# A decoder layer on one core: the last gate/up pair in the wide form, the third block sum behind a split, and turned rows and the last differential head placed later

## Chip, core and metric

The kernel runs on one core of a Trainium2 chip. The metric is the device time of one execution in microseconds (us), the median of three runs. One further execution was taken by the hardware profiler; the profile and the trace are of that one.

## What is computed

One layer, float32, 256 rows of 2048 channels: a half-step SwiGLU feed-forward network (FFN1), a mixer with two attention branches (multi-head latent attention, MLA, with 8 heads, and differential attention with 4 heads), an output projection, and a second FFN. LayerNorm follows each part. Cut to what matters here:

```python
D_MODEL, SEQ, D_FF = 2048, 256, 5632

def _swiglu(x, w_gate, w_up, w_down):
    return (jax.nn.silu(x @ w_gate) * (x @ w_up)) @ w_down

def _mixer(h, ...):
    c_q, c_kv, k_r, dq, dk, dv, gate_mla, gate_diff = _split_columns(h @ w_in)
    q = (_rms_norm(c_q, q_norm_g) @ w_uq)        # 8 heads, 128 plain + 64 turned by _rope
    k_nope, v_mla = c_kv @ w_uk, c_kv @ w_uv     # c_kv after _rms_norm
    o_mla = _mla_attention(q, k, v_mla)          # softmax(q k^T) v, causal
    o_diff = _diff_attention(dq, dk, dv, positions, lam)   # (softmax1 - lam * softmax2) v
    y = sigmoid(gate_mla) * (o_mla @ w_br_mla) + sigmoid(gate_diff) * (o_diff @ w_br_diff)
    return y @ w_out
```

## The kernel before

**Products in three parts.** TensorE (PE) multiplies in a reduced float32 format, so every operand is split in a high and a low part (`split`, L156): ScalarE (ACT) casts the high part (L158), VectorE (DVE) subtracts it for the low part (L159). One product of 128x128 by 128x512 is three matmuls (`triple`, L211: high by high L212, high by low L213, low by high L214). The split weights lie in a ring of six pairs of tiles named `wring`. A unit of work has a load, a preparation (its splits) and its products; loads are issued three units and preparations four units ahead of the products (`look(3, 4)`). `later(n, f)` puts a piece of other work n units behind. The scheduler then decides each engine's order; `tc.issue_after(i)` only keeps an instruction behind another in the order and adds no wait.

**Gate/up.** Each FFN's gate and up weights come in 11 pairs of column blocks of 512, over 16 k tiles of 128. Pair 0 is computed plainly. Pairs 1 to 10 are handled by `Hybrid`: k tiles 0 to 7 are multiplied by a form with seven products in place of eight, which needs sums of weight blocks (DVE, L466, `sraw<-sraw,sraw`; two further sums are made by accumulating DMAs of POOL, L468 and L473) and adds combinations of the activations (tiles `xs`, `xe`, `xm`). The seven products are called forms 1 to 7; forms 6 and 4 need sums on DVE. Each form comes in block 0 and block 1 (two k tiles each) and a third block. In a "narrow" pair the third block is one more k tile (128x512), in a "wide" pair two (128x1024), so that k tiles 8 to 11 too go by seven products. The rest of the k tiles is plain (`p` and `q` units, two k tiles each). The order of forms and plain units is one line of a table:

```python
    ORDERS = {0: "pp5p36np27q4qqq", 1: "p5p36np27q4qq", 2: "5p36np27q4q"}
    PLAIN = {0: ((8, 9), (10, 11), (12, 13), (14, 15)), 1: ((9, 11), (12, 13), (14, 15)), 2: ((12, 13), (14, 15))}
```

(n is form 1 of the next pair). Before the change pairs 2, 3, 4, 6, 7 and 8 are wide. The sum of block 0 is issued with block 0, those of blocks 1 and 2 with block 1, each pinned behind a split already in line (`behind_split`).

**Down.** The gated products `hb` are transposed on DVE in 32x32 blocks (`turn_out`, L771), written to DRAM (`hT`, L773, POOL) and read back as `hraw`; those of pairs 3, 4 and 0 are read back by the SP queue during pair 10 (`get_half`, L1016), and split into `h`. The down projection follows in a similar mixture of sliced forms and plain units.

**Mixer.** Rows are turned to columns through DRAM in the same way: `turn` writes blocks, `wait` units later reads them back (`turned`), and `more` units later uses them; `turn_to_cols` copies with ACT (L795), `turn_to_quad` splits. `qr_done` does this for the rotary part of MLA's q (`qrT`). A differential head has four steps: scores with softmax (L1257 and L1258 are the exponentials, L748 is a square root), `turn` (PE transposes p, L1268), `values`, and `turn2`. Their places among the projections' units are set by `later(2 + 5 * h + 3 * i + i // 3, f)` (L1459). The exponential and the square root lie in different tables of ACT, so changing from one to the other loads a table.

Of the kernel before, what the change touches and what calls it, by code (L numbers as in the profile page):

```python
# [23 lines left out]
KF = DFF // P  # L24
# [4 lines left out]
DH = 4  # L29
# [30 lines left out]
def layer_kernel(ctx: ExitStack, tc: tile.TileContext, a: dict, out: bass.AP):  # L60
# [6 lines left out]
    small = ctx.enter_context(tc.tile_pool(name="small", bufs=1))  # L67
# [4 lines left out]
    def nm(s):  # L72
        uid[0] += 1
        return f"{s}_{uid[0]}"

    def act_tile(shape, dt=F32, name="act"):
        return apool.tile(shape, dt, tag="act", name=nm(name), bufs=SLOTS)

    def tmp_tile(shape, name="tmp", dt=F32):
        return small.tile(shape, dt, tag="tmp", name=nm(name), bufs=6)  # L80
# [26 lines left out]
    def later(n, fn):  # L107
        uid[0] += 1
        heapq.heappush(todo, (step[0] + n, uid[0], fn))
# [45 lines left out]
    cast, lows, fetched, placed, weights = [None], [None], [None], [None], [None]  # L155
# [42 lines left out]
    def unit(load, prep, now, later_on=None):  # L198
        if load is not None:
            load()  # L200
        loaded.append((prep, now, later_on))
        advance(*ahead)

    def next_pair():
        assert len(ring) > len(prepared) + lag[0], (len(ring), len(prepared), lag[0])
        catch_up(len(ring) - 1)
        pair = ring.pop(0)
        ring.append(pair)
        return pair

    def triple(o, xh, xl, wh, wl, first, last, again=False):  # L211
        PE.matmul(o, xh, wh, start=first, stop=False, skip_group_check=again)  # L212
        PE.matmul(o, xh, wl, start=False, stop=False, skip_group_check=again)  # L213
        PE.matmul(o, xl, wh, start=False, stop=last, skip_group_check=again)  # L214
# [139 lines left out]
    def behind_split(n):  # L354
        return tc.issue_after(line[-n].ins) if len(line) >= n else nullcontext()

    def split_in_line(strict, *a):
        with behind_split(1) if strict else nullcontext():
            line.append(split(*a))

    class Hybrid:
# [42 lines left out]
        def group(self, w0, w1, done, wide=0, seeded=False, gates=False):  # L404
            banks = {}
            small = self.small
# [22 lines left out]
            def bank(n):  # L429
                first = n not in banks  # L430
                if first:
                    banks[n] = tr_bank() if n == "Z" and not small else mm_bank()
                return banks[n], first
# [9 lines left out]
            def source(name, s):  # L443
                w, j0 = blocks[name]
                return w[j0 + s] if s < 2 else w[4 + j0 // 2][:, :wide * 512]

            def stored(name, s):
                return R[name][s] if s < 2 else R[name][s][:, :wide * 512]

            def seventh(p, s):  # L450
                load_block, src, add, b = plan[p]
                st = {}
                tiles = G if s < 2 else wide

                def load():
                    if s < 2 and load_block in there:
                        return
                    nc.sync.dma_start(stored(load_block, s), source(load_block, s))

                def prep():  # L460
                    t = stored(src, s)
                    last = None
                    if add is not None:
                        for i in {0: (0,), 1: tuple(range(1, end_s + 1)), 2: ()}[s]:
                            with nullcontext() if small else behind_split(s + 1):
                                last = V.tensor_tensor(out=stored(src, i), in0=stored(src, i), in1=stored(add[1], i), op=ALU.add)  # L466
                    if p == 6 and p in added:
                        nc.gpsimd.dma_start(stored("22", s), source("12", s), accum_op=ALU.add)  # L468
                    pair = [v[:, :tiles * 512] for v in next_pair()]
                    with tc.issue_after(last.ins) if last is not None and not small else nullcontext():  # L470
                        split_in_line(not small, *pair, t)
                    if p == 1 and p in added:
                        nc.gpsimd.dma_start(stored("11", s), source("12", s), accum_op=ALU.add)  # L473
                    st["pair"] = [v.rearrange("p (g n) -> p g n", g=tiles) for v in pair]

                def now():
                    o, first = bank(b)
                    wh, wl = st["pair"]
                    for g in range(tiles):
                        if s < 2:  # L480
                            xh, xl = (v[:, 2 * s + g, :] for v in self.seven.at_[p])
                        else:
                            xh, xl = (v[:, g, :] for v in self.extra.at_[p])
                        triple(o, xh, xl, wh[:, g, :], wl[:, g, :], first and g == 0,
                               s == end_s and g == tiles - 1 and p in stops, b in "XZ" or seeded)
                    if s == end_s and p in after:
                        after[p]()
                unit(load if load_block else None, prep, now)
# [42 lines left out]
            turn = {n: iter(PLAIN[wide]) for n in range(2)}  # L531
# [236 lines left out]
    def turn_out(row, to):  # L768

        t = tmp_tile([P, 512], "blocks")  # L770
        V.transpose(t, row)  # L771
        for i in range(4):
            nc.gpsimd.dma_start(to.rearrange("(g r) (i f) -> i r g f", g=4, i=4)[i],  # L773
                                t[32 * i:32 * (i + 1), :].rearrange("r (g f) -> r g f", g=4))

    def turned(v):
        return v.rearrange("p (i k c) -> p k i c", i=4, k=4)

    def turn(row, use, wait, more):
        to = dram.tile([P, 512], F32, name=nm("turn"))  # L780
        turn_out(row, to)

        def back():
            t = tmp_tile([P, 512], "turned")
            nc.gpsimd.dma_start(t, to)
            later(more, lambda: use(turned(t)))
        later(wait, back)

    def turn_to_quad(row, b, x, q, wait, more):
        turn(row, lambda t: x.put(q, b, t), wait, more)  # L790

    def turn_to_cols(row, dst, b, wait, more, pinned=False):
        def use(t):
            with tc.issue_after(cast[0].ins) if pinned else nullcontext():
                S.copy(dst[:, :, b * P:(b + 1) * P].rearrange("p k (i c) -> p k i c", i=4), t)  # L795
        turn(row, use, wait, more)
# [167 lines left out]
    def ffn(n, x, wgu, wdn, residual, g, bt, each, first=None, between=None, nxt=None, cols=None, norm=None, pending=None):  # L964
# [32 lines left out]
        def sum_done(c, b, bank, snap, op):  # L997
            if snap is None:
                gu_done(c, b, bank)
                return  # L1000
            t = tmp_tile([P, 512], "gus")
            V.tensor_tensor(out=t, in0=bank, in1=snap, op=op)
            half(c, b, t[:, 256:512], t[:, 0:256], 1)
# [60 lines left out]
        def begin():  # L1064
            hy = Hybrid(x, seven, KD, extra=extra, early=early)
            hybrid.append(hy)
            hy.plan([(wgu[2 * p], wgu[2 * p + 1],
                      lambda n, b, bank, snap, op, p=p: sum_done(2 * p + n, b, bank, snap, op),
                      2 if p in (2, 3, 4, 6, 7, 8) else 1, p > 1, ask if p == KF // 4 - 1 else lambda: None)
                     for p in range(1, KF // 4)])  # L1070
        project(wgu[0], x, KD, 512, lambda b, bank: gu_done(0, b, bank), hook=first_hook,
                between=between, norm=norm)
# [17 lines left out]
        for p in range(2):  # L1090
# [30 lines left out]
            else:  # L1121
                call(len(units) - 8, widen)
            down.run(wdn[2 * p], wdn[2 * p + 1], units, forms,
                     lambda m, b, bank, sign, p=p: ln.fold(2 * p + m, b, bank, sign),
                     lambda m, b, bank, p=p: ln.evac(2 * p + m, b, bank), calls, 8 * p)
# [162 lines left out]
    def mixer(x, norm):  # L1288
# [47 lines left out]
        def cols_proj(w, xx, kt, name, k0=0, more=4, pinned=False):  # L1336
            dst = act_tile([P, 4, T], F32, name)

            def done(b, bank):
                t = tmp_tile([P, 512], name + "r")  # L1340
                S.copy(t, bank)
                later(1, lambda: turn_to_cols(t, dst, b, 4, more, pinned))
            project(w, xx, kt, 512, done, k0)
            return dst
# [111 lines left out]

        for h in range(DH):
            for i, f in enumerate(diff_head(h)):
                later(2 + 5 * h + 3 * i + i // 3, f)  # L1459
        qT = [cols_proj(a["wuq"][c], cn, 4, "qT") for c in range(2)]  # L1460
        qrT = act_tile([P, 4, T], F32, "qrT")

        def qr_done(b, bank):
            t = tmp_tile([P, 512], "qr")
            tv = t.rearrange("p (j h i) -> p j h i", j=2, h=MH)
            rope(tv[:, 0], tv[:, 1], bank, b, MH)
            later(1, lambda: turn_to_cols(t, qrT, b, 4, 4))
        project(a["wuq"][2], cn, 4, 512, qr_done)
        kT = [cols_proj(a["wuk"][c], cn, 4, "kT", 4, 6, True) for c in range(2)]
        v = [act_tile([P, 1024], F32, "v") for _ in range(2)]  # L1470
# [211 lines left out]
```

## Time and profile before

| what | us |
|---|---|
| median of 3 runs (lowest to highest) | 1958.54 (1957.15 to 1961.01) |
| the profiled execution, its own time | 1957.34 |
| its span in the trace | 1955.6 |
| PE busy | 1943.0 |
| DVE busy | 1760.4 |
| ACT busy | 1276.4 |
| POOL busy | 377.0 |

The trace gives each instruction its start, its duration and, in brackets, how long its engine had been idle before it and what ended that. Some neighbouring instructions of one line are printed as one row with a count (x3). PE's matmuls are pipelined: each is shown with about 0.39 us, and the next starts before it ends, so what counts there is the distance from start to start. The granted clock of PE was 1.00 throughout. In the order of time, FFN1's gate/up pairs end near 445, its down projection follows, the mixer's attention heads stand between about 1020 and 1110, and FFN2's pair 4 ends near 1471.

### The profile page before, as it was taken

Reading aid. Unit: us, or ns where it says so; the run is one execution under the profiler, and the core shown is the slowest. Engines: PE = TensorE matmul, PEld = TensorE weight load, DVE = VectorE, ACT = ScalarE, POOL = GpSimd, SP = SyncE. Lnnn points to the kernel's source line nnn. Section 1 sums busy time; section 2 is a strip of 40 time slices with the busy share of each in tenths; the row PEclk is TensorE's granted clock in tenths of the full one; section 3 lists DMA queues with packets and bytes.
Section 4 is the critical chain, followed back from the end, with each engine's and each line's share of the span. In section 5 each row is a group of like instructions: output and inputs, shape, how many; then the busy total and the mean of one; then the engine's idle time right before and its main releaser. Section 6 shows DMA issues by size and latency. Waiting matters only on the chain.

```text
span 1955.6 us, 25740 instructions
## 1 busy us (share of the span) xinstructions
PE 1943.0 (99%) x8715; PEld 1609.0 (82%) x8715; DVE 1760.4 (90%) x2117; ACT 1276.4 (65%) x1636; POOL 377.0 (19%) x610
## 2 busy tenths in 40 slices
PE   9999999999999999999999999999999999999998
PEld 8888888888888888888888888888888888888886
DVE  7999999999898879988987677789999999998987
ACT  6677676776655666666667655566767676666652
POOL 0122212321100010102241530012221122210110
PEclk9999999999999999999999999999999999999999
DMA  9988997988877667767676798688988888888973
GB/s 333 295 239 244 271 303 236 239 269 279 313 245 240 215 218 269 262 201 241 198 260 203 221 306 276 200 298 247 252 256 282 279 233 245 274 303 253 320 249 124
DMA packets 152244, 498.30 MB, mean 255 GB/s; under 512 B 22016, under 2 KB 22320, under 8 KB 152112
## 3 DMA queue, kind: packets, MB, share of 16 engines
q1 hardware_dynamic: 110592, 371.64, 52.9%
q0 software_dynamic: 41376, 124.89, 27.2%
q8 instruction: 68, 1.11, 0.2%
q14 instruction: 64, 0.52, 0.1%
q10 hardware_dynamic: 144, 0.13, 0.0%
HBM read 466.16 MB, written 30.41 MB: 254 GB/s over the span
## 4 chain that ended last, share of the span: by engine, by line
PE 94%; DVE 4%; DMA 1%; issue 1%; ACT 0%; SPq 0%; DVEq 0%
PE mm L213 26%; PE mm L214 26%; PE mm L212 26%; PE tr L213 4%; PE tr L214 4%; PE tr L212 4%; DVE wring L159 2%; DVE sraw L466 1%; PE tr L729 1%; DMA sraw<-in_gu_dram 0%; DMA xraw<-in_xT_dram 0%; PE tr L1483 0%; PE tr L1411 0%; PE tr L1485 0%; DMA raw<-in_gu_dram 0%
## 5 line engine op out<-in xcount | busy, mean ns | idle before, releaser
L158 ACT CAST wring<-sraw 128x1024 fp32r<-128x1024 f32 (+1 forms) x576 | 568.2, 1009 | 188.4 <-PE mm L214 69.8
L159 DVE TENSOR_TENSOR wring<-sraw,wring 128x1024 fp32r<-128x1024 f32 (+1 forms) x576 | 651.1, 1165 | 22.1 <-ACT wring L158 19.3
L158 ACT CAST wring<-raw 128x1024 fp32r<-128x1024 f32 (+2 forms) x436 | 448.7, 1035 | 281.2 <-PE mm L214 198.3
L159 DVE TENSOR_TENSOR wring<-raw,wring 128x1024 fp32r<-128x1024 f32 (+2 forms) x436 | 518.3, 1197 | 93.3 <-ACT wring L158 90.7
L212 PE MATMUL mm<-wring,h 128*128 128x512 f32 (+2 forms) x1152 | 443.5, 385 | 0.0
L213 PE MATMUL mm<-wring,h 128*128 128x512 f32 (+2 forms) x1152 | 442.7, 384 | 0.0
L214 PE MATMUL mm<-wring,h 128*128 128x512 f32 (+2 forms) x1152 | 442.6, 384 | 0.0
L212 PEld LDWEIGHTS mm<-wring,h 128*128 128x128 f32 x1152 | 216.4, 188 | 43.0 <-ACT h L158 0.8
L214 PEld LDWEIGHTS mm<-wring,h 128*128 128x128 f32 x1152 | 216.4, 188 | 42.8 <-DVE h L159 0.4
L213 PEld LDWEIGHTS mm<-wring,h 128*128 128x128 f32 x1152 | 216.4, 188 | 42.2
L213 PE MATMUL mm<-wring,xs 128*128 128x512 f32 x616 | 240.2, 390 | 0.5 <-DVE wring L159 0.5
L214 PE MATMUL mm<-wring,xs 128*128 128x512 f32 x616 | 239.7, 389 | 0.0
L212 PE MATMUL mm<-wring,xs 128*128 128x512 f32 x616 | 239.5, 389 | 0.0
L466 DVE TENSOR_TENSOR sraw<-sraw,sraw 128x1024 f32<-128x1024 f32 x168 | 191.4, 1166 | 4.1 <-DMA sraw<-in_wdk_dram 4.0
L773 POOL DMA_DIRECT2D hT<-blocks x176 | 97.5, 561 | 211.1 <-DVE blocks L771 109.4
L213 PEld LDWEIGHTS mm<-wring,xs 128*128 128x128 f32 x616 | 115.6, 188 | 26.0 <-DVE wring L159 2.1
L212 PEld LDWEIGHTS mm<-wring,xs 128*128 128x128 f32 x616 | 115.6, 188 | 24.0
L214 PEld LDWEIGHTS mm<-wring,xs 128*128 128x128 f32 x616 | 115.6, 188 | 23.9
L468 POOL DMA_DIRECT2D sraw<-in_gu_dram x60 | 52.5, 919 | 382.2 <-DVE sraw L466 355.5
L213 PE MATMUL mm<-wring,x 128*128 128x512 f32 x240 | 93.6, 391 | 0.1
L214 PE MATMUL mm<-wring,x 128*128 128x512 f32 x240 | 93.3, 390 | 0.1
L212 PE MATMUL mm<-wring,x 128*128 128x512 f32 x240 | 92.4, 390 | 0.0
(344 smaller groups left out, 2682.6 us busy)
## 6 DMA issues: line engine op xcount, KB each, us to landing
sraw<-in_gu_dram SPq DMA_DIRECT2D x156, 512.0 KB, 7.5
raw<-in_dn_dram SPq DMA_DIRECT2D x140, 512.0 KB, 4.7
raw<-in_gu_dram SPq DMA_DIRECT2D x110, 512.0 KB, 7.2
sraw<-in_gu_dram POOLq DMA_DIRECT2D x104, 512.0 KB, 7.6
sraw<-in_dn_dram SPq DMA_DIRECT2D x36, 512.0 KB, 4.8
raw<-in_w_out_dram SPq DMA_DIRECT2D x32, 512.0 KB, 4.6
hraw<-hT POOLq DMA_DIRECT2D x56, 256.0 KB, 6.2
raw<-in_wgd_dram SPq DMA_DIRECT2D x24, 512.0 KB, 4.4
```

The costliest lines, as they stand in the source:

```text
L158: cast[0] = S.copy(hi, src)
L159: lows[0] = V.tensor_tensor(out=lo, in0=src, in1=hi.bitcast(F32), op=ALU.subtract)
L212: PE.matmul(o, xh, wh, start=first, stop=False, skip_group_check=again)
L213: PE.matmul(o, xh, wl, start=False, stop=False, skip_group_check=again)
L214: PE.matmul(o, xl, wh, start=False, stop=last, skip_group_check=again)
L466: last = V.tensor_tensor(out=stored(src, i), in0=stored(src, i), in1=stored(add[1], i), op=ALU.add)
L468: nc.gpsimd.dma_start(stored("22", s), source("12", s), accum_op=ALU.add)
L729: PE.transpose(t[:, i * P:(i + 1) * P], src[:, i * P:(i + 1) * P], ident)
L773: nc.gpsimd.dma_start(to.rearrange("(g r) (i f) -> i r g f", g=4, i=4)[i], t[32 * i:32 * (i + 1), :].rearrange("r (g f) -> r g f", g=4))
```

## The change

Five edits: the third block sum of a wide pair's forms stands behind one split rather than two (so behind the form's own first split); the splits of `turn_to_quad` and the copy of `qrT` are pinned behind the last cast in line; the `qrT` copy is used 6 rather than 4 units after its read-back; the steps `turn`, `values` and `turn2` of the last differential head come 2, 2 and 1 units later; and gate/up pair 10 becomes wide.

```diff
@@ Hybrid.group, seventh, prep @@
                         for i in {0: (0,), 1: tuple(range(1, end_s + 1)), 2: ()}[s]:
-                            with nullcontext() if small else behind_split(s + 1):
+                            with nullcontext() if small else behind_split(1 if i == 2 and tiles > 1 and wide > 1 else s + 1):
                                 last = V.tensor_tensor(out=stored(src, i), in0=stored(src, i), in1=stored(add[1], i), op=ALU.add)
@@ turn_to_quad @@
     def turn_to_quad(row, b, x, q, wait, more):
-        turn(row, lambda t: x.put(q, b, t), wait, more)
+        def use(t):
+            with tc.issue_after(cast[0].ins), tc.issue_after(lows[0].ins):
+                x.put(q, b, t)
+        turn(row, use, wait, more)
@@ ffn, begin @@
-                      2 if p in (2, 3, 4, 6, 7, 8) else 1, p > 1, ask if p == KF // 4 - 1 else lambda: None)
+                      2 if p in (2, 3, 4, 6, 7, 8, 10) else 1, p > 1, ask if p == KF // 4 - 1 else lambda: None)
@@ mixer @@
         for h in range(DH):
             for i, f in enumerate(diff_head(h)):
-                later(2 + 5 * h + 3 * i + i // 3, f)
+                later(2 + 5 * h + 3 * i + i // 3 + (0, 2, 2, 1)[i] * (h == DH - 1), f)
@@ mixer, qr_done @@
-            later(1, lambda: turn_to_cols(t, qrT, b, 4, 4))
+            later(1, lambda: turn_to_cols(t, qrT, b, 4, 6, True))
```

Over the whole program PE has 8621 matmuls in place of 8627. The lines of the changed kernel stand 3 further down from L790 on.

The first place is ACT's order ahead of differential head 2's exponentials in the mixer. Before the change:

```order
L795 COPY qrT_7822<-turned_8068 128x4x128
L158 CAST wring_110<-raw_8413 128x1024
L158 CAST wring_5032<-raw_8436 128x1024
L795 COPY qrT_7822<-turned_8099 128x4x128
L1257 ACT_TABLE_LOAD
L1257 ACTIVATE p_8149,sums_8150<-st_8142,nmx_8147 128x128
L1258 ACTIVATE p_8149,sums_8150<-st_8142,nmx_8147 128x256
```

And now on ACT, at the same place:

```order
L798 COPY qrT_7809<-turned_8055 128x4x128
L158 CAST wring_114<-raw_8400 128x1024
L158 CAST wring_5019<-raw_8417 128x1024
L1260 ACT_TABLE_LOAD
L1260 ACTIVATE p_8136,sums_8137<-st_8129,nmx_8134 128x128
L1261 ACTIVATE p_8136,sums_8137<-st_8129,nmx_8134 128x256
```

The second copy to `qrT` has left its place ahead of the table load. It stands later on ACT, behind the casts of `od` (differential head 1's output, split):

```order
L748 ACT_TABLE_LOAD
L748 ACTIVATE sd_8195<-oms_8193,floor_72 128x2
L158 CAST wring_116<-raw_8525 128x1024
L158 CAST od_8118<-tr_8293 128x256
L158 CAST od_8122<-tr_8293 128x256
L798 COPY qrT_7809<-turned_8086 128x4x128
L798 COPY kT_7875<-turned_8211 128x4x128
```

So the copy moved behind one square root and its table load, and stands with the copies of `kT`.

The second place is DVE's order in FFN1's gate/up pair 4, form 4: `sraw_428`, `sraw_429` and `sraw_433` are its blocks 0, 1 and 2. Before:

```order
L983 TENSOR_TENSOR hb_1619<-mm_1285,sg_1617 128x256
L466 TENSOR_TENSOR sraw_428<-sraw_428,sraw_388 128x1024
L466 TENSOR_TENSOR sraw_429<-sraw_429,sraw_389 128x1024
L466 TENSOR_TENSOR sraw_433<-sraw_433,sraw_432 128x1024
L159 TENSOR_TENSOR wring_119<-sraw_428,wring_118 128x1024
L159 TENSOR_TENSOR wring_117<-sraw_429,wring_116 128x1024
L159 TENSOR_TENSOR wring_115<-sraw_433,wring_114 128x1024
```

Now, on DVE at the same place:

```order
L986 TENSOR_TENSOR hb_1619<-mm_1285,sg_1617 128x256
L466 TENSOR_TENSOR sraw_428<-sraw_428,sraw_388 128x1024
L466 TENSOR_TENSOR sraw_429<-sraw_429,sraw_389 128x1024
L159 TENSOR_TENSOR wring_119<-sraw_428,wring_118 128x1024
L466 TENSOR_TENSOR sraw_433<-sraw_433,sraw_432 128x1024
L159 TENSOR_TENSOR wring_117<-sraw_429,wring_116 128x1024
L159 TENSOR_TENSOR wring_115<-sraw_433,wring_114 128x1024
```

The third sum and the first split have changed places; the second and third splits stand where they stood.

The third place is DVE's order in FFN1's last pair, form 4 (the same `sraw` tiles; `raw` are plain units, `xs` and `f` over `hraw` belong to the down projection). Before:

```order
L466 TENSOR_TENSOR sraw_428<-sraw_428,sraw_388 128x1024
L983 TENSOR_TENSOR hb_3397<-mm_3058,sg_3395 128x256
L466 TENSOR_TENSOR sraw_429<-sraw_429,sraw_389 128x1024
L159 TENSOR_TENSOR wring_115<-sraw_428,wring_114 128x1024
L466 TENSOR_TENSOR sraw_433<-sraw_433,sraw_432 128x512
L159 TENSOR_TENSOR wring_113<-sraw_429,wring_112 128x1024
L159 TENSOR_TENSOR wring_111<-sraw_433,wring_110 128x512
L159 TENSOR_TENSOR wring_121<-raw_3399,wring_120 128x1024
L159 TENSOR_TENSOR wring_119<-raw_3410,wring_118 128x1024
```

Now, on DVE:

```order
L986 TENSOR_TENSOR hb_3394<-mm_3061,sg_3392 128x256
L466 TENSOR_TENSOR sraw_428<-sraw_428,sraw_388 128x1024
L466 TENSOR_TENSOR sraw_429<-sraw_429,sraw_389 128x1024
L159 TENSOR_TENSOR xs_3463<-hraw_3241,xs_3463 128x256
L583 TENSOR_TENSOR f_3466<-hraw_3241 128x256
L159 TENSOR_TENSOR wring_117<-sraw_428,wring_116 128x1024
L466 TENSOR_TENSOR sraw_433<-sraw_433,sraw_432 128x1024
L159 TENSOR_TENSOR wring_115<-sraw_429,wring_114 128x1024
L159 TENSOR_TENSOR wring_121<-raw_3414,wring_120 128x1024
L159 TENSOR_TENSOR wring_113<-sraw_433,wring_112 128x1024
```

The third sum and the third split are twice as wide, two small operations of the down projection have moved ahead of the form's first split, and a plain unit's split stands ahead of the third. On PE, 14 matmuls stand between form 7's last one and form 4's first L213, where 7 stood.

## The prediction

> **What bounds the kernel now.** I read the page's busy shares first, then its chain, then windows of the stages that the diff touches.
>
> ```profile
> span 1955.6 us, 25740 instructions
> PE 1943.0 (99%) x8715; PEld 1609.0 (82%) x8715; DVE 1760.4 (90%) x2117; ACT 1276.4 (65%) x1636; POOL 377.0 (19%) x610
> PE 94%; DVE 4%; DMA 1%; issue 1%; ACT 0%; SPq 0%; DVEq 0%
> ```
>
> TensorE (PE) is busy for all but 12.6 us of the span, and the chain that ended last is 94% PE. So only two things can move the time: the number of matmuls, and the few places where PE waits. The windows say where those are (columns: stretch, its length, then busy time of PE, PEld, DVE, ACT, POOL with counts, granted clock, DMA share, GB/s).
>
> ```profile
> 166.00:206.00 40.00, 39.73 (x175) 32.28 (x174) 38.85 (x41) 27.92 (x33) 9.63 (x14) 1.00 0.85 253
> 206.00:430.00 224.00, 224.00 (x990) 185.47 (x989) 220.29 (x237) 162.57 (x198) 50.91 (x73) 1.00 0.88 261
> 440.00:490.00 50.00, 50.00 (x222) 41.40 (x221) 49.36 (x64) 31.93 (x42) 9.74 (x18) 1.00 0.81 282
> 490.00:500.00 10.00, 10.00 (x46) 8.27 (x45) 5.49 (x8) 4.69 (x7) 2.00 (x3) 1.00 1.00 340
> 1020.00:1060.00 40.00, 38.85 (x183) 32.07 (x182) 28.15 (x63) 31.63 (x60) 9.96 (x19) 1.00 0.70 223
> ```
>
> From 206 to 430 (gate/up pairs 4 to 10) PE never waits: 224.00 us for 990 matmuls is 0.226 us each, 0.2267 by the starts of neighbouring rows. There the third-sum edit has nothing to win. But VectorE (DVE) stands at 220.29 of 224 as well: PE is the bound by a hair. PE waits 0.27 us before 206 (pair 4) and 1.15 us around 1036 (attention).
>
> **The matmuls.** For two k tiles by seven products the narrow pair issues 7 forms x 5 k tiles x 3 = 105 matmuls and 6 plain units x 12 = 72, together 177; the wide pair 7 x 6 x 3 = 126 and 4 x 12 = 48, together 174. So pair 10 loses 3 matmuls in each FFN, 6 in all. Each stands on the path at 0.2267 us: **-1.36 us**.
>
> **The turned rows.** ACT, PE and DVE around 1036:
>
> ```profile
> 1031.14 0.62 ACT L795 COPY qrT<-turned 128x512 f32<-128x512 f32 x1 [1.50 <-DMA turned<-turn]
> 1031.76 1.28 ACT L1257 ACT_TABLE_LOAD   x1
> 1033.06 0.40 ACT L1257 ACTIVATE p<-st,nmx 128x128 f32<-128x128 f32 x1
> 1034.07 0.17 DVE L1260 RECIPROCAL rs<-sums 128x2 f32<-128x2 f32 x1 [3.18 <-ACT p L1258]
> 1037.36 0.74 DVE L1420 SCALAR_TENSOR_TENSOR p<-p,rs,p 128x128 f32<-128x128 f32 x2
> 1036.32 0.39 PE L214 MATMUL mm<-wring,h 128*128 128x512 f32 x1
> 1037.85 0.30 PE L1268 MATMUL tr<-ident,p 128*128 128x128 f32 x1 [1.15 <-DVE p L1420]
> ```
>
> Before diff head 2's softmax, ACT waits 1.50 us for a row's read-back, then copies it (0.62). Behind it the table load, the exponentials, DVE's products of p and PE's transposes (L1268) follow one another; PE goes from 1036.32 to 1037.85, 1.31 more than a period. The change moves this copy behind the od casts, beside the kT copies, so ACT reaches the table load up to 1.50 + 0.62 = 2.1 us sooner. That is more than 1.31, and what is late next is DVE's max for the softmax, which was ready under the 3.18 us that DVE then waited. Bounds: 0 (another wait takes its place) to -1.31. I take **-1.3**, as one mechanism with 0.8 us to spare.
>
> The later last diff head and the new order cost ACT two more table loads, the exponential and the square root now alternating once more:
>
> ```profile
> L1257 ACT ACT_TABLE_LOAD x5 | 6.4, 1283 | 0.1
> L748 ACT ACT_TABLE_LOAD x3 | 3.8, 1283 | 0.1
> ```
>
> That is 2 x 1.28 = 2.6 us of ACT, of which 31.63 of 40 us are busy in this window. PE there waits for no weight: 38.85 busy and the 1.15 at the transposes make up the 40. So the projections' matmuls hide the loads and I cost them at nothing; if that cover is gone they stand before p's transposes, up to 2.6 us. Less than nothing they cannot cost, since a load does no work. The pinned casts of turn_to_quad change no order that I could find: nothing either way.
>
> A rule speaks against this. The Trainium skill, "ScalarE: Activation LUTs", section "What ACT_TABLE_LOAD costs", gives a switch a load of about 1283 ns and a drain of about 1380 ns. By it the two more would be an estimated 5.3 us of ACT instead of 2.6, still beside PE's work in the forecast. The trace agrees on the load, but the exponential starts at 1033.06, 1.30 us after the load's start, so no drain stands behind it here.
>
> **The third block sum, pair 4.** The starts of PE's rows, and what DVE did:
>
> ```profile
> 200.97 3.48 DVE L466 TENSOR_TENSOR sraw<-sraw,sraw 128x1024 f32<-128x1024 f32 x3
> 204.37 3.48 DVE L159 TENSOR_TENSOR wring<-sraw,wring 128x1024 fp32r<-128x1024 f32 x3
> 204.98 0.39 PE L212 MATMUL tr<-wring,x 128*128 128x512 f32 x1
> 205.64 0.50 PE L213 MATMUL mm<-wring,xs 128*128 128x512 f32 x1 [0.27 <-DVE wring L159]
> 205.97 0.40 PE L214 MATMUL mm<-wring,xs 128*128 128x512 f32 x1
> 184.09 6.36 DVE L159 TENSOR_TENSOR wring<-sraw,wring 128x1024 fp32r<-128x1024 f32 x6
> 184.76 0.61 PE L212 MATMUL mm<-wring,xs 128*128 128x512 f32 x2
> 185.35 0.50 PE L213 MATMUL mm<-wring,xs 128*128 128x512 f32 x1
> 185.69 0.39 PE L214 MATMUL mm<-wring,xs 128*128 128x512 f32 x1
> 1469.71 0.39 PE L212 MATMUL tr<-wring,h 128*128 128x512 f32 x1
> 1470.33 0.50 PE L213 MATMUL mm<-wring,xs 128*128 128x512 f32 x1 [0.23 <-DVE wring L159]
> ```
>
> Form 4: from 204.98 to 205.64 PE loses 0.66 - 0.23 = 0.43, and 0.10 in the slow step after. Form 6 loses 0.14 + 0.11 at 185.35 (two starts of 184.76, 0.2267 apart, a third due at 185.21). The first split waits for three wide sums at (204.37 - 200.97) / 3 = 1.135 us. With the third sum behind it, it ends 1.135 sooner, and both waits at the first split go. The second split, however, ends when it did, 204.37 + 2.27 + 0.08 = 206.72, while PE, now at its L213 from 205.21, wants it 6 matmuls later, at 206.57: 0.2 of form 4's gain comes back as a wait for the second split, with a slow step of 0.11. Form 6's second split ends at 184.09 + 2.35 = 186.44, before its turn at 185.21 + 1.36 = 186.57. Per FFN 0.53 - 0.32 + 0.25 = 0.46; the second FFN shows the same wait (1470.33, 0.39). **-0.9 us** for both; bounds 0 and -1.6 (all of it).
>
> **The wide last pair.** It is paid by DVE. The rows (starts; 418.11 holds two wide and one half sum):
>
> ```profile
> 396.32 1.23 DVE L159 TENSOR_TENSOR wring<-raw,wring 128x1024 fp32r<-128x1024 f32 x1 [1.19 <-ACT wring L158]
> 418.11 2.95 DVE L466 TENSOR_TENSOR sraw<-sraw,sraw 128x1024 f32<-128x1024 f32 x3
> 420.99 2.95 DVE L159 TENSOR_TENSOR wring<-sraw,wring 128x1024 fp32r<-128x1024 f32 x3
> 436.87 1.22 DVE L159 TENSOR_TENSOR wring<-sraw,wring 128x1024 fp32r<-128x1024 f32 x1
> 438.78 0.39 PE L213 MATMUL mm<-wring,xs 128*128 128x512 f32 x1
> L159 DVE TENSOR_TENSOR xs<-hraw,xs 128x256 fp32r<-128x256 f32 x18 | 7.2, 418 | 0.6 <-ACT xs L158 0.6
> 437.72 1.04 ACT L158 CAST wring<-sraw 128x1024 fp32r<-128x1024 f32 x1
> 438.66 0.58 ACT L424 COPY snap<-mm 128x512 f32<-128x512 f32 x1
> 439.14 0.62 ACT L158 CAST wring<-sraw 128x512 fp32r<-128x512 f32 x1
> ```
>
> A half operation costs 420.99 - 418.11 - 2.27 = 0.61, so a third block that becomes whole costs 0.53 more. The narrowest place is form 4, the last: its first split ends at 438.09, and PE wants it at 438.78, **a lead of 0.69**. Ahead of it DVE gets six wider splits and one wider sum (7 x 0.53 = 3.7), loses one plain split (-1.14), and has two quarter-size operations moved ahead (0.42 each by the group's mean, 0.8). DVE's idle 1.19 at 396.32 swallows form 1's 0.53. Sum: +2.8. PE gets 6 more matmuls before that point (18 of six forms, less 12 of the plain unit), and its order now has 14 instead of 7 matmuls between form 7 and form 4's L213: 13 x 0.2267 = 2.95. DVE's lead would stay, at 0.8; the second split, 2.27 behind the first, is wanted 9 matmuls (2.04) after it, and its lead is 0.6.
>
> But ACT is now ahead of DVE there: the cast of that first split stands behind the copy of a bank (L424) that waits for form 7's last matmul. From that matmul's start: 0.39 for itself, 0.48 from the copy's start to the next cast's (438.66 to 439.14), 1.04 for the cast, 1.22 for the split, 3.13 with nothing for the hand-overs; PE wants it 15 matmuls (3.40) later. Four hand-overs share 0.27, and what is late at the first split is late by 0.2 more at the second. I take a wait of 0.3 per FFN, **+0.6**; bounds 0 and 2.2 per FFN (rival 1).
>
> Down, behind it, is where lead could be missing again:
>
> ```profile
> 491.25 0.62 ACT L158 CAST h<-hraw 128x512 fp32r<-128x512 f32 x1 [3.87 <-DMA hraw<-hT]
> 503.77 1.22 DVE L159 TENSOR_TENSOR wring<-raw,wring 128x1024 fp32r<-128x1024 f32 x1
> 506.10 0.39 PE L213 MATMUL mm<-wring,h 128*128 128x512 f32 x1
> ```
>
> At 506.10 the lead is 1.11. But it fell there because ACT waited 3.87 us for a read-back and DVE worked only 5.49 of 10 us; that arrival keeps its place against PE. Nothing, or up to 1.5 where the pair's debt is still there. An FFN loads 256 KB more (five half blocks by load or accumulating DMA, 1280 KB, for two plain units, 1024), at a DMA share of 0.81: nothing, or as much as the read-back is delayed, which the same 1.5 bounds.
>
> **The sum.** -1.36 - 1.3 - 0.9 + 0.6 = -2.96. The profiled execution took 1957.34 us (span 1955.6), so 1954.4. The median of the runs, 1958.54, lies 1.2 above it: **1955.6**.
>
> **Rivals.**
> 1. *DVE's debt in pair 10 is paid by PE; slower.* If the idle time swallows nothing (0.53 more) and the 7 matmuls put ahead must wait as well (1.59 less), form 4's lead is 0.69 - 3.4 + 1.36 = -1.3, and its second split, 2.27 behind with only 6 matmuls (1.36) between, adds 0.9: 2.2 per FFN, 4.4. With 1.5 in each down: 1957.34 - 3.56 + 7.4 = 1961.2, as a median 1962.4. It decides from 1.8 us of wait per FFN (3.56 / 2). For it: DVE 220.29 of 224. Against it: those 7 matmuls need tiles prepared earlier.
> 2. *The wait at 1036 is moved, not removed.* The copy is gone but a later wait, or the two table loads, stands before the transposes: 1955.6 + 1.3 = 1956.9, with both loads 1959.5. For it: ACT is the fuller engine there. Against it: DVE's 3.18 us of idle time.
> 3. *A switch of tables costs ACT more than its load.* If ACT had to stand empty before each added load, as long as the 1.50 us of the row at 1031.14, it would be 3.0 more on rival 2's far end: 1962.5. Against it: the load at 1031.76 starts where the copy ends. The drain of the Trainium skill's page on "ScalarE: Activation LUTs", section "What ACT_TABLE_LOAD costs", would be such a cost, by the page an estimated 2.8.
> 4. *Every wait goes.* -1.36 - 1.3 - 1.6 and nothing in pair 10: 1953.1, as a median 1954.3. For it: the leads come out above zero before the hand-overs.
>
> **How the numbers follow.** Forecast 0.50, rival 1 0.10, rival 2 0.18, rival 3 0.02, rival 4 0.20. About 0.2% (3.9 us) is what a measurement of this kernel can tell from no change: below 1954.6 or above 1962.4. Two thirds of rival 4 and the forecast's lower edge make faster 0.22; the worse half of rival 1, rival 3 and half of rival 2's upper tail make slower 0.10; same 0.68. The range 1953.0 to 1960.5 reaches over rivals 2 and 4 with the runs' own spread of about 1.2, and leaves out rival 3 and the upper part of rival 1.
>
> **What would show it.** Right: PE's count falls by 6; no wait at L1268 near 1036 and none worth naming at its neighbours; L213 at form 4 of pair 4 waits under 0.3; in pair 10 form 4's first L213 waits for DVE by under 1 us. Wrong: waits for `wring` of over 1.8 us around 436 to 445, or a new wait for p or od between 1030 and 1110, or one near 506.

## The result, and the profile after

| | us |
|---|---|
| before, median of 5 runs (lowest to highest) | 1958.34 (1957.15 to 1961.01) |
| after, median of 5 runs | 1966.24 (1965.51 to 1966.90) |
| after to before, ratio with its 95% interval | 1.0039 [1.0027, 1.005] |
| profiled execution after, own time / span | 1965.61 / 1963.8 |

The changed kernel is 7.9 us slower. The forecast was 2.9 us faster, and the time lies outside its range. The page of the changed kernel, beside the lines shown of before (the span, the busy shares, the chain):

```profile
span 1963.8 us, 25707 instructions
PE 1946.8 (99%) x8709; PEld 1605.6 (82%) x8709; DVE 1767.6 (90%) x2113; ACT 1278.1 (65%) x1634; POOL 376.9 (19%) x610
PE 95%; DVE 2%; ACT 1%; DMA 1%; issue 1%; SPq 0%; DVEq 0%; ACTq 0%
```

PE has its 6 matmuls less, and ACT now stands in the chain, where it had 0%. That is the first hint. PE's busy time has grown by 3.8 us although it does less: part of a wait is counted as busy (a matmul ahead of a wait shows its full 0.39, of which the next would overlap 0.16, and the one behind it shows 0.50). The windows of the gate/up stage say where PE stood (columns as in the prediction):

```profile
100.00:166.00 66.00, 65.20 (x287) 53.32 (x286) 63.18 (x63) 45.29 (x53) 19.21 (x28) 1.00 0.87 231
166.00:206.00 40.00, 39.22 (x171) 31.48 (x170) 39.04 (x41) 27.64 (x33) 9.41 (x14) 1.00 0.86 248
206.00:430.00 224.00, 222.84 (x980) 183.20 (x979) 219.24 (x232) 161.30 (x195) 51.07 (x74) 1.00 0.89 265
1020.00:1060.00 40.00, 39.95 (x186) 32.98 (x186) 28.70 (x62) 31.07 (x61) 12.02 (x22) 1.00 0.71 221
```

From 206 to 430, where before had 990 matmuls, after has 980 in the same time. To see it by stage I took the start of the same matmul in both traces and followed how the distance grows:

| stage | after minus before, us |
|---|---|
| FFN1, start to pair 9 (0.17 of it in the first microseconds) | +4.76 |
| FFN1, last pair | -0.37 |
| mixer | -0.76 |
| FFN2, to pair 9 | +4.62 |
| FFN2, last pair (-0.4) and down (+0.4) | -0.03 |
| sum (the spans differ by 8.2) | +8.22 |

So the loss lies in the gate/up pairs, 4.6 us in each FFN, and up to pair 9 the third-sum edit is the only one that acts there. The mixer's -0.76 can't be put down to its edits by this table: over the same stage experiment 1 below comes to -0.85 and experiment 2 to +2.6, and both have the mixer of before. Form 6 in pair 3, where before had no wait, on PE:

```profile
145.49 0.61 PE L212 MATMUL mm<-wring,xs 128*128 128x512 f32 x2
146.29 0.50 PE L213 MATMUL mm<-wring,xs 128*128 128x512 f32 x1 [0.18 <-DVE wring L159]
147.55 0.39 PE L212 MATMUL mm<-wring,xs 128*128 128x512 f32 x1
148.56 0.50 PE L213 MATMUL mm<-wring,xs 128*128 128x512 f32 x1 [0.62 <-DVE wring L159]
```

And on DVE, first before the change, then after:

```profile
139.91 3.49 DVE L466 TENSOR_TENSOR sraw<-sraw,sraw 128x1024 f32<-128x1024 f32 x3
143.31 6.90 DVE L159 TENSOR_TENSOR wring<-sraw,wring 128x1024 fp32r<-128x1024 f32 x6
```

```profile
141.83 2.35 DVE L466 TENSOR_TENSOR sraw<-sraw,sraw 128x1024 f32<-128x1024 f32 x2
145.01 1.23 DVE L159 TENSOR_TENSOR wring<-sraw,wring 128x1024 fp32r<-128x1024 f32 x1 [0.83 <-ACT wring L158]
146.15 1.22 DVE L466 TENSOR_TENSOR sraw<-sraw,sraw 128x1024 f32<-128x1024 f32 x1
147.28 1.22 DVE L159 TENSOR_TENSOR wring<-sraw,wring 128x1024 fp32r<-128x1024 f32 x1
148.80 2.36 DVE L159 TENSOR_TENSOR wring<-sraw,wring 128x1024 fp32r<-128x1024 f32 x2 [0.29 <-ACT wring L158]
```

At 147.55 PE goes on only at 148.56: 1.01 instead of 0.23. What matters is the bracket at 145.01: **DVE itself stands 0.83 us, for a cast of ACT**. ACT's row there:

```profile
142.97 5.79 ACT L158 CAST wring<-sraw 128x1024 fp32r<-128x1024 f32 x6 [3.01 <-PE tr L214]
```

Six casts in one row. By the order of the instructions the first of them is not of the form's first block but of `sraw_428`, a block of the next pair's form 1; the form's own two follow (`sraw_279`, `sraw_280`), and its third block's cast (`sraw_430`) is the last of the six. Before, the form's first two blocks were cast first, and its third block fourth. Stands like this one, ahead of a form's first or third block, are spread over the wide pairs; the group of these splits on DVE shows them together (busy, mean ns, idle time ahead of them and its releaser), before and after:

```profile
L159 DVE TENSOR_TENSOR wring<-sraw,wring 128x1024 fp32r<-128x1024 f32 (+1 forms) x576 | 651.1, 1165 | 22.1 <-ACT wring L158 19.3
```

```profile
L159 DVE TENSOR_TENSOR wring<-sraw,wring 128x1024 fp32r<-128x1024 f32 (+1 forms) x576 | 661.7, 1177 | 32.3 <-ACT wring L158 29.7
```

That is 10.2 us more of idle time over the whole program, on an engine that works 220 of 224 us in the gate/up stage.

### The profile page after: what moved, and what is told of

Same layout as the page of the kernel before. It is cut to its first block, busy times and chain, and to the rows that moved or that the text cites. A ratio compares the mean times of both kernels' runs of the same rounds, so it can differ in the third digit from the quotient of the medians.

```text
span 1963.8 us, 25707 instructions
## 1 busy us (share of the span) xinstructions
PE 1946.8 (99%) x8709; PEld 1605.6 (82%) x8709; DVE 1767.6 (90%) x2113; ACT 1278.1 (65%) x1634; POOL 376.9 (19%) x610
## 4 chain that ended last, share of the span: by engine, by line
PE 95%; DVE 2%; ACT 1%; DMA 1%; issue 1%; SPq 0%; DVEq 0%; ACTq 0%
PE mm L213 27%; PE mm L214 27%; PE mm L212 27%; PE tr L213 4%; PE tr L214 4%; PE tr L212 4%; DVE wring L159 1%; ACT wring L158 1%; PE tr L729 1%; DMA xraw<-in_xT_dram 0%; DVE sraw L466 0%; PE tr L1486 0%; PE tr L1414 0%; PE tr L1488 0%; DMA raw<-in_dn_dram 0%
## 5 line engine op out<-in xcount | busy, mean ns | idle before, releaser
L158 ACT CAST wring<-sraw 128x1024 fp32r<-128x1024 f32 (+1 forms) x576 | 572.3, 1020 | 198.9 <-PE mm L214 96.3
L159 DVE TENSOR_TENSOR wring<-sraw,wring 128x1024 fp32r<-128x1024 f32 (+1 forms) x576 | 661.7, 1177 | 32.3 <-ACT wring L158 29.7
L159 DVE TENSOR_TENSOR wring<-raw,wring 128x1024 fp32r<-128x1024 f32 (+2 forms) x432 | 513.0, 1196 | 87.0 <-ACT wring L158 84.9
L213 PE MATMUL mm<-wring,h 128*128 128x512 f32 (+2 forms) x1148 | 441.2, 385 | 0.0
L213 PEld LDWEIGHTS mm<-wring,h 128*128 128x128 f32 x1148 | 215.7, 188 | 42.2
L213 PE MATMUL mm<-wring,xs 128*128 128x512 f32 x616 | 242.1, 393 | 5.5 <-DVE wring L159 5.5
L213 PEld LDWEIGHTS mm<-wring,xs 128*128 128x128 f32 x616 | 115.6, 188 | 37.3 <-DVE wring L159 13.5
L213 PE MATMUL mm<-wring,x 128*128 128x512 f32 x236 | 92.0, 391 | 0.5 <-DVE wring L159 0.4
L214 PE MATMUL mm<-wring,x 128*128 128x512 f32 x236 | 91.8, 390 | 0.0
L212 PE MATMUL mm<-wring,x 128*128 128x512 f32 x236 | 90.9, 390 | 0.1
```

The source lines that it names most:

```text
L158: cast[0] = S.copy(hi, src)
L159: lows[0] = V.tensor_tensor(out=lo, in0=src, in1=hi.bitcast(F32), op=ALU.subtract)
```

## The experiments

Three theories stood at first. **C**: ACT's changed order of casts makes DVE stand, and PE pays the debt. **D**: the sum between the splits makes the second split late in itself, whatever ACT does. **L**: the wide last pair's load on DVE is the cause. Times are against the kernel before on the same chip; medians of 5 to 11 runs.

### 1. The third-sum edit alone

```diff
-                            with nullcontext() if small else behind_split(s + 1):
+                            with nullcontext() if small else behind_split(1 if i == 2 and tiles > 1 and wide > 1 else s + 1):
```

> The kernel before with the third-sum edit alone. Theory C (ScalarE's order): with the sum between the splits, casts of other blocks come ahead of the form's own cast on ScalarE, VectorE stands 0.8 us for it per form, and the debt of several wide pairs falls on TensorE in pairs 3, 4 and 8: 4.6 us per FFN in the changed kernel's trace, so +9 us here. Theory D (dependency: the second split itself ends too late, whatever ScalarE does): +9 us as well. Theory L (the wide last pair's load is what costs): within 1 us of before.

Measured: 1967.74 against 1958.57, ratio 1.0045 [1.0032, 1.0057]: +9.2 us. L falls: the whole loss comes without a wide last pair.

### 2. The third-sum edit, with ACT's casts pinned

The pins add an edge in ACT's order and no wait. The source is otherwise that of experiment 1. In the built programs some 70 of ACT's instructions stand elsewhere than in experiment 1, and on DVE nine; but the scheduler has also moved 16 of PE's matmuls and 14 of SP's loads by some places, so the orders of these two are not quite equal.

```diff
+    fence = [None]
     def split_in_line(strict, *a):
         with behind_split(1) if strict else nullcontext():
-            line.append(split(*a))
+            with tc.issue_after(fence[0].ins) if strict and fence[0] is not None else nullcontext():
+                line.append(split(*a))
...
                         split_in_line(not small, *pair, t)
+                    if add is not None and not small and wide > 1 and s == end_s:
+                        fence[0] = cast[0]
```

> The kernel before with the third-sum edit, and in wide pairs every later unit's cast pinned behind the cast of the form's third block, so that ScalarE takes the form's blocks first. Theory C: VectorE's stands of 0.8 us go and the time is within 1.5 us of before (0 to -1 if pair 4's wait goes too). Theory D: at least half of the loss stays, +4.5 us or more. Theory L: within 1 us of before, as without the pins.

Measured: 1956.24 against 1958.57, ratio 0.9991 [0.9982, 1.0]: -2.3 us, 11.5 us away from experiment 1. Form 6 of pair 3 on DVE, in this kernel (its sums are at L470):

```profile
140.41 2.35 DVE L470 TENSOR_TENSOR sraw<-sraw,sraw 128x1024 f32<-128x1024 f32 x2
142.74 1.23 DVE L159 TENSOR_TENSOR wring<-sraw,wring 128x1024 fp32r<-128x1024 f32 x1
143.89 1.22 DVE L470 TENSOR_TENSOR sraw<-sraw,sraw 128x1024 f32<-128x1024 f32 x1
145.02 5.89 DVE L159 TENSOR_TENSOR wring<-sraw,wring 128x1024 fp32r<-128x1024 f32 x5
```

The sum stands between the splits exactly as in the changed kernel, and no bracket is left: DVE goes through. D falls, C stands: the sum's place by itself costs nothing; what costs is the casts' order that came with it. The loss of 9.2 was more than made good, which C had put at 0 to -1, but the interval against before reaches 1.0.

### 3. The changed kernel without the third-sum edit

```diff
-                            with nullcontext() if small else behind_split(1 if i == 2 and tiles > 1 and wide > 1 else s + 1):
+                            with nullcontext() if small else behind_split(s + 1):
```

> The changed kernel without the third-sum edit (the other four edits stay). Theories C and D: the loss goes and what stays is the mixer's gain of 0.8 and the last pair's 0 to 0.4: -1 us against before (-2 to 0). Theory L: +3 us or more.

Measured: 1956.97 against 1958.57, ratio 0.9991 [0.9982, 0.9999]: -1.6 us. The other four edits together are a small gain.

### 4. The wide last pair alone

```diff
-                      2 if p in (2, 3, 4, 6, 7, 8) else 1, ...
+                      2 if p in (2, 3, 4, 6, 7, 8, 10) else 1, ...
```

> The kernel before with gate/up pair 10 wide alone. Theories C and D: 6 matmuls less at 0.2267 us is -1.36, less the waits of form 4 (0.3 to 0.6 per FFN in the changed kernel): -0.4 us (-1.4 to +0.5). Theory L: +3 us or more.

Measured: 1958.60 against 1958.57, ratio 1.0003 [0.9994, 1.0011]: no difference. In its trace the last pair gains 0.50 in each FFN by the same-matmul distance, and FFN2's down gives some of it back, at a place where before had no wait:

```profile
1727.42 0.39 PE L212 MATMUL tr<-wring,xs 128*128 128x512 f32 x1
1728.28 0.50 PE L213 MATMUL tr<-wring,xs 128*128 128x512 f32 x1 [0.48 <-DVE wring L159]
```

0.86 instead of 0.23. This trace says more: its mixer is that of before, and at the transposes near 1036 PE hardly waits (0.33 us from start to start, where before has 1.53). Instead it waits at a place that in the profile of before had no wait:

```profile
1178.80 0.39 PE L214 MATMUL mm<-wring,om 128*128 128x512 f32 x1
1180.25 0.63 PE L729 MATMUL tr<-ident,diff 128*128 128x128 f32 x4 [1.06 <-DVE diff L1537]
```

### 5. All edits, with the casts pinned

The changed kernel with the diff of experiment 2, whose core is:

```diff
+            with tc.issue_after(fence[0].ins) if strict and fence[0] is not None else nullcontext():
+                line.append(split(*a))
```

> The changed kernel with all its edits, and the casts pinned as in the second experiment. If theory C is the whole cause, the parts add up: -2.3 us of the third sum with pins, -0.9 of the last pair by its trace, 0 to -0.8 of the mixer: -3.5 us against before (-2.3 to -4.5). If something else in the changed kernel costs time beside the third sum: above -1.5.

Measured: 1956.28 against 1957.97, ratio 0.9992 [0.9983, 1.0001]: -1.7 us, outside the -2.3 to -4.5 that was expected. The changed kernel's 7.9 us are gone, but the parts do not add up. Its trace shows 1.6 us (1725.94 to 1727.53, 1.36 lost) at the same place of FFN2's down as experiment 4.

### 6. The pins alone

The kernel before with the diff of experiment 2, and without that of experiment 1:

```diff
                             with nullcontext() if small else behind_split(s + 1):
...
+                    if add is not None and not small and wide > 1 and s == end_s:
+                        fence[0] = cast[0]
```

> The kernel before with the pins alone; the three sums stand ahead of the first split as they did. If the gain of the second experiment is that of the sum's new place (the waits at pair 4's first splits), the pins alone give 0 (-0.6 to +0.6). If it is that of the casts' order, about -2 us here too.

Measured: 1957.01 against 1957.97, ratio 0.9997 [0.9988, 1.0006]: -1.0 us, between the two cases and not clear of zero. The trace is plainer than the time: both waits of pair 4 are gone although three sums still stand ahead of the first split.

```profile
166.00:206.00 40.00, 40.00 (x178) 33.00 (x177) 40.00 (x42) 29.30 (x35) 9.60 (x14) 1.00 0.88 259
```

PE is busy for all 40 us where before had 39.73, and DVE for all 40.00 where it had 38.85. At form 6 of pair 4 the first split ends 0.51 sooner than in before, and that alone removes the wait. At form 4 the scheduler has also put three matmuls (0.68) ahead of the first L213, so there the run does not part the two. By the same-matmul distance it gains 0.74 in FFN1 and 0.80 in FFN2; experiment 2, with the sum moved as well, 0.94 and about 0.85.

### 7. The mixer's edits alone

The pins of `turn_to_quad` as in the change, and:

```diff
-                later(2 + 5 * h + 3 * i + i // 3, f)
+                later(2 + 5 * h + 3 * i + i // 3 + (0, 2, 2, 1)[i] * (h == DH - 1), f)
...
-            later(1, lambda: turn_to_cols(t, qrT, b, 4, 4))
+            later(1, lambda: turn_to_cols(t, qrT, b, 4, 6, True))
```

> The kernel before with the mixer's edits alone (turned rows behind casts, the later copy of qrT, the last differential head later). If they remove a wait that stands in every execution: -1.3 us. If the 1.15 us at 1036 was one execution's read-back (the fourth experiment, with the mixer of before, shows no wait there and one of 1.06 at 1179): 0 to -0.8.

Measured: 1957.17 against 1957.97, ratio 0.9997 [0.9988, 1.0006]: -0.8 us, not clear of zero.

### 8. The third-sum edit in pairs 2 and 6 alone

Each is the first of three wide pairs in a row.

```diff
+            alone = self.pair in (2, 6)
...
-                            with nullcontext() if small else behind_split(s + 1):
+                            with nullcontext() if small else behind_split(1 if i == 2 and tiles > 1 and wide > 1 and alone else s + 1):
```

> The kernel before with the third-sum edit in the first wide pair of each row alone (2 and 6), without pins. If VectorE's stands are a debt that TensorE pays only where the lead is used up: about 1.7 us of debt in pair 2 against a lead of 1.0 in pair 3, so 0.7 per FFN and nothing behind pair 6: +1.4 us (0 to +2.5). If each stand of 0.8 is paid where it stands, two forms in two pairs in two FFNs: +6 us.

Measured: 1960.36 against 1957.97, ratio 1.0011 [1.0002, 1.002]: +2.4 us, near the upper end of the debt's range and far from 6. In the trace pair 2 itself has no wait; by the same-matmul distance PE pays 1.2 in each FFN in pair 3, whose sums stand as before, gets 0.3 of it back at pair 4's waits, and pays nothing at pair 7. Here a stand of DVE is paid one pair later, and only where the lead has run out.

### 9. All edits but the wide last pair, with the casts pinned

```diff
-                      2 if p in (2, 3, 4, 6, 7, 8, 10) else 1, ...
+                      2 if p in (2, 3, 4, 6, 7, 8) else 1, ...
```

> The changed kernel with the casts pinned and gate/up pair 10 narrow as before. If the last pair's gain (0.47 per FFN in gate/up) is given back in FFN2's down (a wait of 0.5 to 1.2 at 1726 in two traces): the same as the fifth experiment within 0.7, some -2.5 us against before (-1.5 to -3.5). If the last pair is a gain: 1 us slower than the fifth.

Measured: 1955.65 against 1957.95, ratio 0.999 [0.9981, 0.9999]: -2.3 us. This fits the first case: beside experiment 5's -1.7 the narrow last pair loses nothing, so the wide one brings nothing that shows. It is the only version here, beside experiment 3, whose interval lies below 1. Whether it is better than experiment 2, 3 or 5 these runs cannot tell.

### 10. Pins behind the second block instead of the third

Experiment 2, changed so that others may stand ahead of the third block's cast:

```diff
-                    if add is not None and not small and wide > 1 and s == end_s:
+                    if add is not None and not small and wide > 1 and s == 1:
```

> The kernel before with the third-sum edit, the later casts pinned behind the cast of the form's second block, not the third, so that another block's cast may still stand ahead of the third's. In the first experiment's FFN1, VectorE stands 3.9 us for third blocks and 3.1 for first ones between 95 and 390. If both kinds cost: the first kind goes, half of the third kind's stays as debt, +1 to +4 us against before. If only a cast ahead of the first block costs: -2 us, as in the second experiment.

Measured: 1969.74 against 1957.95, ratio 1.0058 [1.0045, 1.0071]: +11.8 us, more than either case. (The two sums in the expectation are the wrong way round: 3.3 us were for third blocks and 4.0 for first ones.) DVE in pair 2, form 6:

```profile
103.93 1.22 DVE L470 TENSOR_TENSOR sraw<-sraw,sraw 128x1024 f32<-128x1024 f32 x1
105.06 1.22 DVE L159 TENSOR_TENSOR wring<-sraw,wring 128x1024 fp32r<-128x1024 f32 x1
107.12 3.50 DVE L159 TENSOR_TENSOR wring<-sraw,wring 128x1024 fp32r<-128x1024 f32 x3 [0.84 <-ACT wring L158]
```

The stand is now at the third block, in ten of FFN1's twelve wide forms with sums. Its cast can start only when the moved sum ends, at 105.15; ACT then has another block's cast in hand. Between the sum and the third split DVE has one split of 1.135 to do, which covers one cast (1.05) and not two. The cast ahead of the third block is thus at least as dear as the one ahead of the first.

One table puts the runs on sums and casts side by side: DVE's idle time in FFN1 from 95 to 390 (every idle time over 0.12 us, summed) and the time against before.

| kernel | DVE idle, us | time against before, us |
|---|---|---|
| experiment 2, sum moved, pinned | 1.4 | -2.3 |
| experiment 9 | 1.4 | -2.3 |
| experiment 6, pins alone | 2.7 | -1.0 |
| before | 3.5 | 0 |
| experiment 8, sum moved in pairs 2 and 6 | 4.1 | +2.4 |
| experiment 1, sum moved | 7.9 | +9.2 |
| experiment 10, pins at the second block | 8.3 | +11.8 |

From before to experiment 1, DVE idles 4.3 us more in one FFN and PE loses 4.6 in each. The order of the rows holds throughout, the sizes only roughly: in FFN1 experiment 10 idles 4.7 more and loses 5.6 by the same-matmul distance, experiment 2 idles 2.1 less and gains 0.9.

## Why the prediction was wrong, step by step

**The third block sum: this step failed.** The prediction put it at -0.9 us with bounds of 0 and -1.6, and said that from 206 to 430 the edit "has nothing to win". It could lose there, and no loss was priced: of FFN1's 4.6 us, 1.9 are lost in that stretch (pair 8) and 2.7 ahead of it, in pairs 3 and 4. The step followed DVE's order alone, took the splits to run one behind the other at 1.135, and showed DVE's rows of pair 4. A split needs its cast as well, and the scheduler had given ACT a new order of casts in the wide pairs. Experiments 1 and 2 show that this order is the loss. The text had the warning in hand: DVE at 220.29 of 224 "by a hair" means that idle time of DVE soon becomes a debt to PE. It was used to say that PE was the bound, not to ask what would make DVE stand.

**Pair 4's waits were misread too.** The prediction explained them by three sums ahead of the first split. Experiment 6 leaves the sums there and the waits go. Their source lies one pair earlier, in a row of before that wasn't read, where DVE waits for ACT between form 4's second and third split; in experiment 6 this wait is gone:

```profile
167.65 1.23 DVE L159 TENSOR_TENSOR wring<-sraw,wring 128x1024 fp32r<-128x1024 f32 x1 [1.15 <-ACT wring L158]
```

**The matmuls** were right: 6 fewer. **The wide last pair** was near in size and not in place: a wait of 0.3 per FFN was forecast at form 4's first L213, and 0.68 - 0.37 = 0.31 is what FFN1 of the changed kernel shows. But that L213 does not stand out (446.64, 0.25 after the matmul ahead of it); the 0.31 is spread over slow steps between 445.15 and 449.04, so that the two figures agree is in part luck. And the part on down, costed at nothing "or up to 1.5", did come: in three of the four traces with a wide last pair (not in experiment 3's) there is 0.2 to 1.4 of wait in FFN2's down (behind 1727.42 in experiment 4, 0.63), none in FFN1's, and the pair alone measures no gain. Rival 1, the forecast's mechanism for a slower kernel, looked for the debt here; the mechanism (DVE's debt is paid by PE) was the right one, at the wrong place.

**The turned rows.** A wait of 1.31 was to go. In the changed kernel it went almost wholly:

```profile
1040.75 0.39 PE L214 MATMUL mm<-wring,h 128*128 128x512 f32 x1
1041.19 0.30 PE L1271 MATMUL tr<-ident,p 128*128 128x128 f32 x1
```

0.44 in place of 1.53. The mechanism was right: in the seven traces with the mixer of before, ACT's wait for the read-back ahead of the second copy to `qrT` is 0.29 to 2.27, and in six of them PE's step at these transposes is 0.03 or 0.04 longer than that wait (1.50 and 1.53 in before). The size was that of one execution. The step is 1.27 in the mean of the seven and 0.45 in the mean of the five with the changed mixer, so by an estimate from these traces the edits are worth 0.8 at this place, and not 1.3. The edits alone measure -0.8 too, with an interval around zero. Other waits of the mixer move as much, with the old mixer and the new: the step ahead of the transposes of `diff` near 1180 is 1.45 in experiment 4 and 1.81 in experiment 9. So a wait that the arrival of a read-back ends was priced from one execution, as if it stood in every one. The two added table loads are in the trace, at their 1.28 each:

```profile
L1260 ACT ACT_TABLE_LOAD x6 | 7.7, 1283 | 0.1
L748 ACT ACT_TABLE_LOAD x4 | 5.1, 1283 | 0.1
```

They do not stand in the window from which the prediction took their cover (1020 to 1060) but behind it, the exponential's at 1064.84 and the square root's at 1069.49. PE waits for neither: it is busy for 19.94 of the 20 us from 1060 to 1080. So rival 3 did not come. Rival 2 came in part at most: 0.28 of the 1.09 won at the transposes is lost again by 1100. Nor does a drain show at the loads: the idle time ahead of each group's loads is 0.1 us in all, and in the prediction's row the exponential starts 1.30 us after its load. The Trainium skill's page "ScalarE: Activation LUTs" (section "What ACT_TABLE_LOAD costs") adds a drain of about 1380 ns to every switch of tables; here the measurement decides against it.

**What stays open.** Why the scheduler's order of casts changes in some pairs and not in others was not traced. What moves the read-backs' arrival in the mixer was not traced either. The small parts (mixer, last pair, the sum's new place with pins) are each within about 1 us, and experiment 5 shows that they do not simply add.

## What to carry to other kernels

When two engines feed a third and the second is nearly as full as the third, price a reordering by the idle time that it gives the second: follow every input of the moved instruction, and compare the order on each engine that makes one, not only on the engine that was edited. An edge that holds one engine's order lets the scheduler rearrange its neighbours; if the order there matters, pin it as well. A wait that ends with a DMA's arrival should be priced from several executions.

## What was not expected of the hardware

Nothing new in the engines themselves. What surprised was how nearly DVE's stands turn into PE's time once its lead is gone: 4.3 us more of idle time in one FFN, 4.6 us of loss in each (experiment 1). And how much the read-backs' arrival moves from trace to trace: PE's wait at the transposes near 1036 took, in kernels whose mixer is the same, 1.15 us (before), none that the trace marks (experiment 4), 1.92 (experiment 2) and 1.41 (experiment 10, whose row this is):

```profile
1044.10 0.30 PE L1274 MATMUL tr<-ident,p 128*128 128x128 f32 x1 [1.41 <-DVE p L1426]
```
